# Scheduling the RWKV recurrence steps ahead of all other ready work in a two-block fp32 kernel

## The chip, the cores and the metric

The kernel runs on one core of a Trainium2 chip. The metric is the device time of one execution in microseconds (us). Before the change the median of three runs is 2998.11 us (2994.8 to 3004.18). About 0.3%, 9 us, is what a measurement of this kernel can tell from no change.

## The reference

One launch computes two transformer-like blocks on a 256 x 1024 fp32 input `x`. The first block is: a SwiGLU feed-forward, a mixing stage, and a second SwiGLU. Its mixing stage is what matters here:

```
h = rms_norm(x, mix_norm)
p_rwkv, p_q, p_k, p_v, p_gate = split(h @ w_in)
y_a = rwkv7_time_mix(p_rwkv, ...)          # 16 heads of 64, a recurrence over 256 steps:
                                           #   state = state*w + (state@a) b^T + v k^T ; out = state @ r
y_b = dilated_attention(p_q, p_k, p_v)     # 3 groups of 4 heads
merged = g_a * (y_a @ w_proj_rwkv) + g_b * (y_b @ w_proj_attn)     # g = sigmoid(p_gate + b_gate)
x = x + merged @ w_out
```

The second block has two layers, each with three branches (mLSTM, differential attention, Fourier) and a SwiGLU. All their modulation rows come from products `silu(c) @ w_ada`; those of its first layer are computed during the first block's mixing stage.

## The kernel before

Every large matrix product goes through weight blocks. `weights` (line 194) loads a block `wr` of 128 x 1024 or 128 x 512 numbers from HBM by a DMA in the queue of SP (SyncE), ScalarE (ACT) rounds it to `wh` (line 201), VectorE (DVE) forms the rest `wl = wr - wh` (line 202), and TensorE (PE) multiplies three times: by lines 213 to 215 into `g` where tokens are the rows of the result, by lines 248 to 250 where tokens are its columns. A block of the first kind feeds 12 matmuls. There are four buffers of `wr` and three each of `wh` and `wl`.

In the mixing stage `first_block` (line 994 and below) builds generators, each a piece of work cut into steps by `yield`. The string PLAN names the generator whose next step is written out: "0" and "1" are the two halves (8 heads each) of the RWKV recurrence, "k" the keys, receptances and values of the second half, "a" the dilated attention, "g" the gates, "r" the modulation rows (`ada`, line 1105, which multiplies `wa`, 512 KB each).

A half's recurrence is a chain. `rwkv_prep`: decay products (`pz`, `pa`, `pl`, `px`, `pe`, lines 543 to 565), elementwise work on DVE (lines 575 to 603: `kk`, `XA`, `eL`, `em`, `bon`), copies to `WV` and `GB` by 20 small DMAs (lines 612 to 617), transposes `tr` (line 626) with their copies `AR` and `BK`. `rwkv_solve`: products `gr` (line 666) masked into `GB` on DVE (lines 671, 673), four transposes `FS` (line 686), 31 rounds of forward substitution on DVE (`fsp` line 695, `T` line 697), products `pq` and `pr2` (lines 713, 718), and for each of two token tiles `p` (lines 767, 777, 792), the state products `pf` (lines 817, 819), normalisation and the gate product `pg` (lines 750, 751). Token shifts (`pv`, `pr`, lines 475 to 477) precede each half.

PLAN does not fix the order in which an engine executes. The program's layer has a scheduler that walks the written program: of the instructions that are ready by its own reckoning it takes the one with the smallest priority number, which is normally the place in the written program. The result is one fixed queue for each engine, in which an instruction that waits holds up all behind it; PE and SP likewise. The rows of such queues are shown below for the change.

## Time and profile before

| what | value |
|---|---|
| median of three runs | 2998.11 us |
| the profiled execution's own time | 2999.31 us |
| its span, first to last instruction | 2997.5 us |
| PE busy, matmuls | 2890.7 us, 96% |
| PE busy, weight loads | 2429.5 us, 81% |
| DVE, ACT busy | 1775.0 us, 59%; 1178.6 us, 39% |
| data moved by DMA | 409.57 MB, mean 137 GB/s |
| mixing stage's recurrences | about 253 to 613 us of the span |

A row of a timeline begins with its start in us from the span's start and its length; a value in square brackets is how long the engine sat idle before it, and what ended that. `PEclk` is the share of full speed that TensorE was granted. The trace records a matmul of these fp32 products as two entries, so that `x4` in a timeline of PE is two instructions.

### The profile page before, as it was taken

How to read it: one execution, taken by the hardware profiler on the slowest of the kernel's cores; microseconds unless marked ns; L12 is line 12 of the kernel's file. 1: busy time of each engine (PE TensorE's matmuls, PEld its weight loads, DVE VectorE, ACT ScalarE, POOL GpSimd, SP SyncE). 2: the span in 40 equal slices, each digit the busy share in tenths (PEclk: the TensorE clock that was granted, in tenths of full speed). 3: DMA queues.
4: the chain of work that ended last, by engine and by line, in shares of the span. 5: the costliest groups of instructions: out<-in, count | busy, mean ns of one | idle time of the engine just before them, and what ended most of it. 6: DMA issues, size and time to landing. Idle time of an engine off the chain costs nothing.

```text
span 2997.5 us, 42457 instructions
## 1 busy us (share of the span) xinstructions
PE 2890.7 (96%) x16704; PEld 2429.5 (81%) x16704; DVE 1775.0 (59%) x3036; ACT 1178.6 (39%) x1943; POOL 98.4 (3%) x265
## 2 busy tenths in 40 slices
PE   8999999998999999999999999999999999999998
PEld 7987676767997888987788987877778897799797
DVE  5557847446555445436784266777665555665665
ACT  4444333334443334325442333222344444444443
POOL 1010000002000000000000001000020000000000
PEclk9999989889999999999999999999999999999999
DMA  6656737346664222231233254555442243255564
GB/s 199 188 160 202 237 117 216 101 144 206 185 186 127 64 71 64 72 104 51 64 118 105 85 169 146 159 173 155 148 140 85 85 140 101 78 152 169 169 189 141
DMA packets 291441, 409.57 MB, mean 137 GB/s; under 512 B 30757, under 2 KB 182181, under 8 KB 291242
## 3 DMA queue, kind: packets, MB, share of 16 engines
q1 hardware_dynamic: 291242, 406.87, 44.5%
q8 instruction: 131, 2.15, 0.3%
q14 instruction: 68, 0.56, 0.1%
HBM read 396.98 MB, written 3.24 MB: 134 GB/s over the span
## 4 chain that ended last, share of the span: by engine, by line
PE 82%; DVE 8%; issue 3%; ACT 3%; POOL 2%; DMA 2%; SPq 0%; ACTq 0%; POOLq 0%; DVEq 0%
PE g L214 12%; PE g L215 11%; PE g L213 11%; PE g L248 10%; PE g L250 10%; PE g L249 10%; DVE wl L202 2%; PE dC L1363 2%; PE tr L316 1%; PE ada L1105 1%; PE I L1339 1%; ACT dae L1460 1%; PE pf L817 1%; PE f L1530 1%; PE pf L819 1%
## 5 line engine op out<-in xcount | busy, mean ns | idle before, releaser
L202 DVE TENSOR_TENSOR wl<-wr,wh 128x1024 fp32r<-128x1024 f32 (+1 forms) x606 | 733.6, 1212 | 717.3 <-ACT wh L201 714.8
L201 ACT CAST wh<-wr 128x1024 fp32r<-128x1024 f32 (+1 forms) x606 | 630.8, 1042 | 1061.0 <-PE g L215 494.5
L214 PE MATMUL g<-wl,xh 128*128 128x512 f32 (+2 forms) x1880 | 733.2, 390 | 12.5 <-DVE wl L202 12.5
L213 PE MATMUL g<-wh,xh 128*128 128x512 f32 (+2 forms) x1880 | 731.1, 392 | 9.6 <-ACT wh L201 5.8
L248 PE MATMUL g<-xh,wh 128*128 128x256 f32 (+1 forms) x2352 | 726.7, 309 | 3.8 <-ACT wh L201 3.1
L215 PE MATMUL g<-wh,xl 128*128 128x512 f32 (+2 forms) x1880 | 727.6, 388 | 0.0
L250 PE MATMUL g<-xh,wl 128*128 128x256 f32 (+1 forms) x2352 | 722.8, 307 | 1.9 <-DVE wl L202 1.9
L249 PE MATMUL g<-xl,wh 128*128 128x256 f32 (+1 forms) x2352 | 723.1, 307 | 0.0
L248 PEld LDWEIGHTS g<-xh,wh 128*128 128x128 f32 x2352 | 452.8, 193 | 34.7 <-issue 6.7
L250 PEld LDWEIGHTS g<-xh,wl 128*128 128x128 f32 x2352 | 452.5, 192 | 30.5 <-issue 7.3
L249 PEld LDWEIGHTS g<-xl,wh 128*128 128x128 f32 x2352 | 452.9, 193 | 26.5 <-issue 7.0
L214 PEld LDWEIGHTS g<-wl,xh 128*128 128x128 f32 x1880 | 359.2, 191 | 90.6 <-DVE wl L202 20.3
L213 PEld LDWEIGHTS g<-wh,xh 128*128 128x128 f32 x1880 | 357.1, 191 | 88.3 <-ACT wh L201 9.7
L215 PEld LDWEIGHTS g<-wh,xl 128*128 128x128 f32 x1880 | 358.8, 191 | 74.7 <-issue 5.7
L1155 DVE SCALAR_TENSOR_TENSOR aa<-wa,cond,aa 128x512 f32<-128x512 f32 x168 | 114.8, 744 | 4.0 <-DMA wa<-in_w_ada_dram 4.0
L303 ACT CAST xh<-tr 128x256 fp32r<-128x256 f32 (+1 forms) x114 | 50.4, 462 | 131.7 <-PE tr L316 116.2
L1460 ACT ACTIVATE dae<-sc,dast 128x512 f32<-128x512 f32 (+1 forms) x96 | 58.5, 614 | 42.2 <-DVE dast L1458 37.3
L304 DVE TENSOR_TENSOR xl<-tr,xh 128x256 fp32r<-128x256 f32 (+1 forms) x114 | 57.5, 529 | 22.6 <-ACT xh L303 22.2
L1458 DVE TENSOR_REDUCE dast<-sc 128x1 f32<-128x512 f32 (+1 forms) x96 | 53.8, 596 | 24.2 <-PE sc L1457 23.8
L316 PE MATMUL tr<-ident,hn 128*128 128x128 f32 x160 | 28.7, 316 | 39.6 <-DVE hn L345 20.2
L316 PEld LDWEIGHTS tr<-ident,hn 128*128 128x128 f32 x160 | 22.4, 163 | 47.6 <-DVE hn L343 20.6
L330 POOL TENSOR_SCALAR rn_s<-rn_s 128x1 f32<-128x1 f32 x20 | 11.2, 560 | 1209.8 <-ACT junk L329 849.0
(392 smaller groups left out, 2676.9 us busy)
## 6 DMA issues: line engine op xcount, KB each, us to landing
wr<-in_w_in_dram SPq DMA_DIRECT2D x156, 512.0 KB
wr<-in_ffn_w_in_dram SPq DMA_DIRECT2D x88, 512.0 KB
wr<-in_w_ffn_in_dram SPq DMA_DIRECT2D x84, 512.0 KB
wr<-in_w_in_dram SPq DMA_DIRECT2D x156, 256.0 KB
wr<-in_w_ffn_out_dram SPq DMA_DIRECT2D x50, 512.0 KB
wa<-in_w_ada_dram SPq DMA_DIRECT2D x48, 512.0 KB
wa<-in_w_ada_dram SPq DMA_DIRECT2D x96, 256.0 KB
wr<-in_ffn_w_out_dram SPq DMA_DIRECT2D x44, 512.0 KB
```

What stands on the lines that cost most here:

```text
L201: nc.scalar.copy(out=wh[:, :kn, :ntot], in_=src)
L202: nc.vector.tensor_tensor(out=wl[:, :kn, :ntot], in0=src, in1=wh[:, :kn, :ntot].bitcast(F32), op=ALU.subtract)
L213: nc.tensor.matmul(o_, xh, wh[:, n0:n1], start=(kc == 0), stop=False)
L214: nc.tensor.matmul(o_, xh, wl[:, n0:n1], start=False, stop=False)
L215: nc.tensor.matmul(o_, xl, wh[:, n0:n1], start=False, stop=(kc == nk - 1))
L248: nc.tensor.matmul(o_, wh[:, fs], xh, start=(kc == 0), stop=False)
L249: nc.tensor.matmul(o_, wh[:, fs], xl, start=False, stop=False)
L250: nc.tensor.matmul(o_, wl[:, fs], xh, start=False, stop=(kc == nk - 1))
L316: self.nc.tensor.transpose(p[:, j * P:(j + 1) * P], src[:, (c + j) * P:(c + j + 1) * P], self.ident)
L1155: nc.vector.scalar_tensor_tensor(out=y, in0=raw, scalar=self.cond[:, k, s:s + 1], in1=acc[s], op0=ALU.mult, op1=ALU.add)
L1363: nc.tensor.matmul(pc[:, 0:257], kw[:, kc * P:(kc + 1) * P], V[t][:, 0:257], start=True, stop=True)
L1460: nc.scalar.activation(out=em, in_=ps[:, 0:n], func=AF.Exp, bias=st[:, m:m + 1], scale=1.0, accum_out=st[:, 2 + m:3 + m])
```

## The change

Each step of the generators "0" and "1" is written out under `high_priority()`, which sets the priority number to that of the program's start for the instructions emitted inside it and restores it afterwards. Nothing is computed differently. Lines behind the edit are numbered two higher in the changed kernel.

```
             for x in PLAN:
-                next(fills[x], None)
+
+                with self.tc.high_priority() if x in "01" else ExitStack():
+                    next(fills[x], None)
```

Each engine has the same instructions as before. The sequence of the weight blocks (`wr`, `wh`, `wl`, 606 of each) is the same on SP, ACT and DVE. Only what stands between them moves, and only in one piece: on PE about 1500 instructions from matmul number 1426 on, up to the first half's last transposes, on DVE about 500. Everything before and after stands as it did. Counted in weight blocks that DVE has split before it, no step of a recurrence moves by more than five places: the first half's `GB` (line 671) from 90 to 87, its 19th round of substitution from 94 to 89, its `TB` (line 701) stays at 100, the second half's first round of substitution stays at 118, and the last state update (line 829) stays at 129.

DVE, first half, from the end of the key norm (`kn_y`) to the end of the elementwise chain. Before:

```order
L202 TENSOR_TENSOR wl<-wr,wh 128x1024
L297 SCALAR_TENSOR_TENSOR kn_y<-kn_w,kn_y 128x16
L582 TENSOR_TENSOR kk<-kk,kn_y 128x1024
L585 SCALAR_TENSOR_TENSOR XA<-kk,ex 128x512 x2
L202 TENSOR_TENSOR wl<-wr,wh 128x1024
L587 SCALAR_TENSOR_TENSOR kk<-ta,kk 128x1024
L629 COPY AR<-tr 128x8x64
L589 SCALAR_TENSOR_TENSOR kk<-kk,em 128x1024
L590 SCALAR_TENSOR_TENSOR ta<-ta,kar 128x1024
L202 TENSOR_TENSOR wl<-wr,wh 128x1024 x2
```

The same place after:

```order
L202 TENSOR_TENSOR wl<-wr,wh 128x1024
L295 TENSOR_TENSOR kn_w<-kn_y 128x16
L296 SCALAR_TENSOR_TENSOR kn_w<-kn_w,n_2410 128x16
L297 SCALAR_TENSOR_TENSOR kn_y<-kn_w,kn_y 128x16
L582 TENSOR_TENSOR kk<-kk,kn_y 128x1024
L475 TENSOR_TENSOR pv<-pv,pr 128x1024
L585 SCALAR_TENSOR_TENSOR XA<-kk,ex 128x512 x2
L476 TENSOR_TENSOR pv<-pv,mu 128x1024
L587 SCALAR_TENSOR_TENSOR kk<-ta,kk 128x1024
L477 TENSOR_TENSOR pr<-pr,pv 128x1024
L589 SCALAR_TENSOR_TENSOR kk<-kk,em 128x1024
L590 SCALAR_TENSOR_TENSOR ta<-ta,kar 128x1024
```

The weight block that stood inside the chain now stands behind it, and the token shift of the values (lines 475 to 477), which stood ahead of it, runs inside it.

SP, first half, where the copies to `WV` and `GB` and the loads `wa` stand. Before:

```order
L194 DMA wr<-in_w_in_dram 128x2x512 x4
L612 DMA WV<-pr 64x512 x4
L194 DMA wr<-in_w_in_dram 128x2x256
L616 DMA GB<-kk 64x4x64 x8
L194 DMA wr<-in_w_in_dram 128x2x256
L617 DMA GB<-em 64x4x64 x8
L1101 DMA wa<-in_w_ada_dram 128x1024 x2
```

After, from the last loads that stand ahead of the copies:

```order
L194 DMA wr<-in_w_in_dram 128x2x512 x3
L612 DMA WV<-pr 64x512 x2
L616 DMA GB<-kk 64x4x64 x4
L612 DMA WV<-pr 64x512
L616 DMA GB<-kk 64x4x64 x2
L612 DMA WV<-pr 64x512
L617 DMA GB<-em 64x4x64 x6
```

Three weight loads that stood ahead of the ten loads `wa` (92 before them in all) now stand behind them (89). In the second half two more weight loads than before stand ahead of the copies.

PE, first half, the state products of the first 64-step chunk of the second token tile. Before, its eight pairs of `pf` stand behind `pg` and follow each other with nothing between (the rows show the first pair):

```order
L750 MATMUL pg<-g_3198,lg 128x512
L751 MATMUL pg<-g2b,lg 128x512
L817 MATMUL pf<-WV,GB 128x64
L819 MATMUL pf<-S,RG 128x64
```

After, six weight matmuls stand between the first four pairs (the rows begin with the last of them) and the other four:

```order
L817 MATMUL pf<-WV,GB 128x64
L819 MATMUL pf<-S,RG 128x64
L250 MATMUL g<-xh,wl 128x256
L248 MATMUL g<-xh,wh 128x256
L249 MATMUL g<-xl,wh 128x256
L250 MATMUL g<-xh,wl 128x256
L248 MATMUL g<-xh,wh 128x256
L249 MATMUL g<-xl,wh 128x256
L817 MATMUL pf<-WV,GB 128x64
```

What follows moves too: 58 weight matmuls stand directly behind the eighth pair, where 3 did. Behind the attention's transposes that come next stand 72, where 12 did; the second chunk's pairs come after those.

## Rows read from the trace of the kernel before

**Rows 1.** The page: the span, and each engine's busy time.
```profile
span 2997.5 us, 42457 instructions
PE 2890.7 (96%) x16704; PEld 2429.5 (81%) x16704; DVE 1775.0 (59%) x3036; ACT 1178.6 (39%) x1943; POOL 98.4 (3%) x265
```

**Rows 2.** Windows, the recurrences' stretch: length, busy by engine, PEclk, DMA share, GB/s.
```profile
253.00:613.00 360.00, 345.06 (x2215) 248.38 (x2214) 238.41 (x538) 126.48 (x240) 3.81 (x11) 0.89 0.54 164
```

**Rows 3.** Waits of PE in 253 to 613 us: total, times, longest.
```profile
PE g L214 <- DVE wl L202: 6.0, 4, 2.8
PE g L213 <- ACT wh L201: 5.3, 4, 2.2
...
PE pq L713 <- DVE drs_w L296: 0.8, 1, 0.8
```

**Rows 4.** Windows inside that stretch, columns as in rows 2.
```profile
265.00:280.00 15.00, 10.83 (x43) 8.25 (x42) 11.19 (x21) 7.25 (x10) 0.00 (x0) 0.77 0.78 263
280.00:320.00 40.00, 39.26 (x238) 27.14 (x240) 38.03 (x63) 10.72 (x17) 1.64 (x4) 1.00 0.75 227
320.00:330.00 10.00, 5.43 (x33) 4.60 (x26) 8.94 (x27) 2.90 (x5) 0.42 (x1) 0.83 0.61 191
...
380.00:400.00 20.00, 20.00 (x96) 12.23 (x95) 7.61 (x11) 7.01 (x13) 0.00 (x0) 0.74 0.35 112
...
420.00:455.00 35.00, 35.00 (x157) 25.97 (x156) 16.50 (x39) 8.55 (x15) 0.00 (x0) 0.71 0.28 77
455.00:485.00 30.00, 28.88 (x179) 20.99 (x175) 24.77 (x45) 7.13 (x13) 0.00 (x0) 1.00 0.68 203
485.00:500.00 15.00, 12.01 (x46) 6.88 (x46) 14.35 (x57) 6.13 (x11) 0.00 (x0) 0.89 0.55 184
...
550.00:613.00 63.00, 62.94 (x344) 44.15 (x344) 28.38 (x83) 17.24 (x47) 0.20 (x4) 0.73 0.23 76
```

**Rows 5.** Timeline of DVE in the first half.
```profile
279.80 1.23 DVE L582 TENSOR_TENSOR kk<-kk,kn_y 128x1024 f32<-128x1024 f32 x1
281.06 1.29 DVE L585 SCALAR_TENSOR_TENSOR XA<-kk,ex 128x512 f32<-128x512 f32 x2
...
298.68 0.41 DVE L671 TENSOR_TENSOR GB<-gr,kbase 128x256 f32<-128x256 f32 x1
...
305.60 3.72 DVE L686 STREAM_TRANSPOSE FS<-GB 32x1024 f32<-32x1024 f32 x3
...
316.47 0.19 DVE L695 TENSOR_TENSOR fsp<-FS,T 128x30 f32<-128x30 f32 x1
...
324.75 0.29 DVE L695 TENSOR_TENSOR fsp<-FS,T 128x128 f32<-128x128 f32 x1
```

**Rows 6.** Timeline of PE in the first half.
```profile
270.04 0.73 PE L213 MATMUL g<-wh,xh 128*128 128x512 f32 x2 [2.24 <-ACT wh L201]
272.71 0.79 PE L214 MATMUL g<-wl,xh 128*128 128x512 f32 x1 [1.93 <-DVE wl L202]
...
282.04 0.60 PE L626 MATMUL tr<-ident,XA 128*128 128x128 f32 x4
...
283.15 0.40 PE L213 MATMUL g<-wh,xh 128*128 128x512 f32 x1
...
286.33 0.40 PE L215 MATMUL g<-wh,xl 128*128 128x512 f32 x1
...
307.15 1.03 PE L1105 MATMUL ada<-wa,cond 128*2 128x512 f32 x4 [0.69 <-DMA wa<-in_w_ada_dram]
...
322.44 0.50 PE L213 MATMUL g<-wh,xh 128*128 128x256 f32 x2 [1.81 <-ACT wh L201]
...
325.69 0.58 PE L214 MATMUL g<-wl,xh 128*128 128x256 f32 x1 [2.75 <-DVE wl L202]
```

**Rows 7.** Timelines of SP's queue and of ACT around the loads `wa`.
```profile
304.02 9.84 SPq L1101 DMA_DIRECT2D wa<-in_w_ada_dram  x8
313.92 27.41 SPq L194 DMA_DIRECT2D wr<-in_w_in_dram  x16
...
321.77 1.32 ACT L201 CAST wh<-wr 128x512 fp32r<-128x512 f32 x2 [5.53 <-DMA wr<-in_w_in_dram]
```

## The prediction

> **What bounds the kernel now.** I read the page's busy times first: TensorE's matmuls cover 96% of the span and no other engine comes near [rows 1]. So time is won only where TensorE waits or runs slowly. The change reorders one piece, so next I read a window over the stretch in which that piece executes, 253 to 613 us [rows 2]. TensorE is busy for 345.06 of its 360 us: 14.9 us idle. Its mean granted clock is 0.89, so about 360 x 0.11 = 39.6 us went to the lower clock. These two numbers, 54 us together, are all that any order of the same instructions could give back.
>
> The waits of TensorE in that stretch say what it waits for [rows 3]: 11.3 of the 14.9 us are for weight blocks, `wl` from VectorE (6.0) and `wh` from ScalarE (5.3). A recurrence's own product (`pq`, by a step that shares VectorE with it) accounts for 0.8. TensorE therefore does not wait for the recurrence; it waits for the weight stream that shares VectorE with it. That decides the case: work on the recurrence's chain is given an order that it hardly lacked, at the cost of the stream that does bound.
>
> The windows show where the 39 us of clock lie [rows 4]. Each loses its length times (1 - clock): 3.5 (265 to 280), 1.7 (320 to 330), 5.2 (380 to 400), 10.2 (420 to 455), 1.7 (485 to 500), 17.0 (550 to 613), 39.2 in all. Three of them (6.8 us) hold idle TensorE. The other 32.4 us fall where TensorE is busy throughout with `pf`, `p`, one-row and two-column products, small work of the recurrences and of `ada`.
>
> **The Trainium skill on the clock.** "TensorE: Matmul & The Clock Gate", section "HAM oscillation — how this bites in real kernels", says that gaps in which TensorE idles bring the lower clock, and that matmuls should stay back to back. The trace agrees for 6.8 us and not for 32.4 us, where there is no gap to name. By the rule alone each new wait of some us would add a fall like that of 320 to 330 us and nothing could be won elsewhere; that speaks against this change.
>
> **The change part by part.** No instruction is added, so the sum holds only waits and clock.
>
> *The end.* The last steps of the second half stand where they did in the weight stream, and so does everything behind them. The chain is not what the next stage waits for: both orders end the stretch at the same matmul. That term is 0.
>
> *268 to 275 us.* TensorE waits 2.24 us for `wh` and 1.93 for `wl` [rows 6]. In the new order the square `sq` goes ahead of two of ScalarE's exponentials, and one 1024-wide token-shift operation no longer stands ahead of the first `wl`. A 1024-wide operation takes 1.23 us [rows 5]. I take 1.2 off the second wait and 0.5 off the first: -1.7. Bounds: 0 and -4.2.
>
> *The elementwise chain.* Between three weight blocks and the next, VectorE now executes seven 1024-wide operations, two 512-wide ones and three short ones: 7 x 1.2 + 1.2 + 3 x 0.2 (the 30-element step took 0.19) = 10.2, and 1.2 for the next `wl`: 11.4 us [rows 5]. TensorE has cover for part of it. A block is 12 matmuls at 0.227 us (14 steps from 283.15 to 286.33) = 2.7 us [rows 6]. Three blocks are 8.2, of which 2.4 pass while the later two are split; eight transposes take 0.9 (282.04 to 283.15 less one matmul), and two matmuls of the next block, which need `wh` only, 0.5. That is 7.2 us, so a new wait for `wl` of about 4 us, near 280 us. Bounds: 0 (the prep runs sooner than I think) and 10.
>
> *The substitution.* Before, TensorE waits 0.69, 1.81 and 2.75 = 5.25 us between 307 and 326 us [rows 6]. The cause is in the queue of SyncE: the weight loads go behind eight `wa` (9.84 us of issue), and the first arrives 7.9 us after the queue reaches it, at 321.77 [rows 7]. Now three weight loads more stand behind `wa`. The `wa` themselves start some 4 us sooner, so the first block behind them should land near 317 us and TensorE meets VectorE instead. There the `BK` copies of the second tile stand behind four pairs of `GB` masks (8 x 0.41 = 3.3 us), for which `gr` waits about 3 us. Then come four `FS` (1.24 each), during which `gr`, `ada` and one block cover. Then 17 rounds without a weight block: 15 took 8.28 us from 316.47 to 324.75, so 9.4; with two 1024-wide shifts ahead (2.4), two short steps (0.4) and the `wl` (1.2), 13.4 us [rows 5]. Against it stand ten matmuls (2.3), twelve `ada` at 0.5 (1.03 for two) and two of the next block, 8.9 us [rows 6]: a wait of 4.5. So 7.5 for 5.25: +2.3. Bounds: -5.25, and +8.4 if the twelve `ada` (6.2) arrive too late to cover.
>
> *The first `pq`.* 27 more weight matmuls stand ahead of it, so its wait of 0.8 [rows 3] goes: -0.8.
>
> *The second half.* Its steps keep their places to within three blocks. The windows 455 to 500 us hold 1.1 + 3.0 = 4.1 us of idle [rows 4]; two weight loads more stand ahead of the copies, for which I take -1.5 (0 to -4.1).
>
> *The clock.* In 420 to 455 us, 10.2 us were lost. There 58 and 72 dense weight matmuls now stand in blocks between the small products. I take 4 of it, between 0 (the same small products come in some order anyway) and 10.2. The new wait near 280 us costs a fall like that of 320 to 330: +1.7. Of the 17.0 and 5.2 I take nothing, since the runs of `pf`, `p` and `pz` there are much the same in both orders.
>
> Sum: -1.7 + 4.0 + 2.3 - 0.8 - 1.5 - 4.0 + 1.7 = 0.0. So the profiled execution's 2999.31 us stays; it is 1.2 above the median of the runs shown, 2998.1, which is therefore the forecast: 2998 us.
>
> **The rivals.**
>
> *The weight stream starves (slower).* One mechanism: VectorE is a fixed queue, and the chain put first in it delays `wl`. For it: the three waits above, and VectorE is busy 38.0 us of the 40 before 320 us [rows 4], so nothing is caught up there. Price: the elementwise wait at its upper bound (+6 over what I took) and the substitution's at its own (+6.1), and no gain of 4 from the clock: about +16, 3014 us. It decides once TensorE's waits between 265 and 330 us, now 4.2 + 5.25 = 9.4, pass some 20. Against it: `ada` and the transposes lie beside the chain. The skill's rule, by which each of these waits brings a fall of the clock, would add 2 to 3 falls at 1.7 us.
>
> *The small products are spread out (faster).* For it: most of the clock's loss sits on runs of small products without a gap, and the first half's `pf` are now split by weight matmuls. If 420 to 455 us keep the full clock and half of the 17.0 of 550 to 613 goes, the clock gives 18.7 in place of 4: about -15, 2983 us. Against it: the second half's order hardly changes.
>
> *The change does next to nothing.* The scheduler took the recurrences' steps almost as soon as they were ready before; no step moves by more than five weight blocks and most by none or one. Then every term above is near 0 and the time is 2998 us, the same as the forecast's.
>
> **How the numbers follow.** Under 0.3%, 9 us, a measurement of this kernel cannot tell. The forecast has 0.40 and the change that does nothing 0.14, both within it. The spread of small products has 0.24, for the clock holds the largest sum and no row tells how it would answer. The starved stream has 0.22. So faster 0.24, the same 0.54, slower 0.22. The range takes in both rivals but for their far ends: 2982 to 3013 us. The forecast's own range is 2990 to 3006.
>
> **What would show it.** Right: matmul idle of 13 to 18 us in the recurrences' stretch; a wait of `g` for `wl` near 280 us of about 4 us; the one behind the substitution named `wl` and not a DMA; a mean clock of 0.88 to 0.92 in the stretch; and the stretch 360 us long within 8. Wrong: idle over 25 us there (the stream starves), or a clock above 0.93 (the small products matter more than I take), or any difference that arises after 613 us, where both orders are one.

## The result and the profile after

The changed kernel takes 3028.44 us, the median of 6 runs (3015.54 to 3035.81). The kernel before takes 3000.9 us beside it (6 runs, 2994.8 to 3006.43). The ratio is 1.0085 with an interval of 1.0066 to 1.0103: 27 us slower. The forecast was 2998 us in a range that ends at 3013 us, so it missed.

The profiled execution took 3035.81 us, near the slow end of its runs. The page's first lines answer to [rows 1]:

```profile
span 3034.0 us, 42452 instructions
PE 2916.3 (96%) x16704; PEld 2442.4 (81%) x16704; DVE 1777.3 (59%) x3036; ACT 1178.3 (39%) x1943; POOL 98.3 (3%) x265
```

The span grew by 36.5 us against [rows 1]. TensorE's busy time grew by 25.6 us with the same 16704 instructions in it. More busy time for the same instructions means that they ran more slowly. The clock records of the traces show two levels, full (2.4 GHz) and half (1.2 GHz). The mean granted clock, first before and then after:

```profile
core 0: 2997.5 us, clock 0.975
core 0: 3034.0 us, clock 0.966
```

So 3034.0 x 0.0336 = 102 us went to the lower clock against 75 before (clocks to four digits from these records): 27 of the 36.5 us.

The next rows are windows of the changed kernel, first over the whole stretch (253 to 644 us answers to 253 to 613 in [rows 2]), then inside it, as in [rows 4]. Columns: start and end, length, busy time and instructions of PE, PEld, DVE, ACT, POOL, then PEclk, DMA share, GB/s.

```profile
253.00:644.00 391.00, 369.44 (x2226) 261.28 (x2227) 241.56 (x538) 127.13 (x241) 3.82 (x11) 0.84 0.49 151
268.00:280.00 12.00, 9.60 (x41) 7.10 (x40) 9.92 (x19) 8.07 (x12) 0.00 (x0) 0.86 0.87 285
320.00:335.00 15.00, 9.88 (x51) 8.02 (x48) 12.16 (x38) 5.43 (x8) 0.00 (x0) 0.77 0.41 115
...
420.00:440.00 20.00, 20.00 (x93) 17.26 (x93) 5.71 (x11) 3.98 (x7) 0.00 (x0) 0.66 0.30 97
437.10:454.20 17.10, 15.94 (x125) 13.57 (x124) 10.14 (x24) 9.31 (x14) 0.00 (x0) 1.00 0.56 158
450.00:480.00 30.00, 28.84 (x103) 20.58 (x102) 15.54 (x30) 7.60 (x15) 0.00 (x0) 0.60 0.43 121
516.00:573.00 57.00, 54.80 (x488) 37.92 (x486) 40.11 (x109) 24.21 (x56) 1.04 (x2) 1.00 0.59 182
573.00:590.00 17.00, 17.00 (x81) 10.42 (x80) 5.38 (x12) 1.23 (x4) 0.00 (x0) 0.60 0.37 121
607.00:644.00 37.00, 37.00 (x147) 28.83 (x147) 15.66 (x46) 10.32 (x27) 0.20 (x4) 0.54 0.04 15
```

The stretch, up to the same matmul in both, is 31 us longer. TensorE is idle for 21.6 us of it against 14.9: +6.7. Its mean clock is 0.84 against 0.89: 391 x 0.16 = 62.6 us lost against 39.6, +23. From 516 to 573 us the clock is at its full level, so the loss sits in separate places, among them 450 to 480 us (30 x 0.40 = 12 us), 573 to 590 (6.8) and 607 to 644 (17.0). In the last two TensorE has no idle time at all: 17.00 us busy of 17.00, 37.00 of 37.00.

The longest of TensorE's waits in the stretch answer to [rows 3]; the columns are the same:

```profile
PE g L214 <- DVE wl L202: 5.4, 3, 3.4
PE g L213 <- ACT wh L201: 4.5, 3, 2.1
PE ada L1107 <- DMA wa<-in_w_ada_dram: 4.1, 3, 2.8
PE tr L882 <- DVE dsq L875: 3.1, 2, 1.7
PE pz L543 <- DMA w<-in_rwkv_w_dram: 1.4, 1, 1.4
```

Waits for `wl` and `wh` are 11.0 us in all with 1.1 us at line 250, against 11.5 before (11.3 and 0.2 at line 250): no more than there were. The waits for `wa` loads grew from 1.1 to 4.1 us. New are the 1.3 us in which `gr` waits for `BK`, the wait at the first `pz` and those for `dsq` (before, `tr` waited 1.2 us for another step of VectorE).

The last piece of the second half's recurrence shows what happens inside a low place. Two timelines of PE (start, duration, instruction). First the kernel before, behind its third `pg`:

```profile
577.54 0.43 PE L819 MATMUL pf<-S,RG 64*128 64x64 f32 x2
577.90 1.59 PE L1105 MATMUL ada<-wa,cond 128*2 128x512 f32 x4
579.42 0.69 PE L817 MATMUL pf<-WV,GB 128*128 128x64 f32 x2
...
583.13 1.87 PE L1105 MATMUL ada<-wa,cond 128*2 128x512 f32 x4
...
592.87 0.43 PE L817 MATMUL pf<-WV,GB 128*128 128x64 f32 x2
```

Such a group of `pf` takes 0.43 us at the full clock and 0.69 at the lower one. The clock falls at 578 us, and `ada` stands twice between the `pf`. By 592 us `pf` takes 0.43 us again. Now the changed kernel, at the same place:

```profile
607.46 0.44 PE L819 MATMUL pf<-S,RG 64*128 64x64 f32 x2
607.83 0.69 PE L817 MATMUL pf<-WV,GB 128*128 128x64 f32 x2
...
611.53 1.89 PE L1107 MATMUL ada<-wa,cond 128*2 128x512 f32 x8
...
617.36 0.69 PE L819 MATMUL pf<-S,RG 64*128 64x64 f32 x2
...
627.06 0.69 PE L819 MATMUL pf<-S,RG 64*128 64x64 f32 x2
```

Sixteen of these groups follow each other without `ada`, which comes as a block of eight entries behind them; two sets of eight `pf` groups follow, with `sc`, `tr`, `po` and a few weight matmuls between. The clock falls at 607.8 us, and at 627 us `pf` still takes 0.69 us. By the clock records the lower level lasts here until 641.9 us, 34.1 us at a stretch; before, the same work had 13.7 and 10.2 us with 3.4 us at the full clock between.

Six other orders of the next section pass the same place, one profile each. With sixteen groups ahead of `ada`, as here, the lower level lasts 27.3 us (second half only; steps behind the solve). With eight groups ahead of the first `ada` and `ada` twice between, it lasts 30.7 us (steps to the solve; all others) and 37.5 us (with `ada`'s steps). With six groups ahead of it, as before, it lasts 10.2 us (first half only). So `ada` between the groups is not enough for a short fall; the short ones go with the six groups ahead of the first. That is read from these traces and not tested.

### The profile page after: what moved, and what is told of

The parts are those of the page before. It is cut to its first block, busy times and chain, and to the rows that moved or that the text cites. A ratio compares the mean times of both kernels' runs of the same rounds, so it can differ in the third digit from the quotient of the medians.

```text
span 3034.0 us, 42452 instructions
## 1 busy us (share of the span) xinstructions
PE 2916.3 (96%) x16704; PEld 2442.4 (81%) x16704; DVE 1777.3 (59%) x3036; ACT 1178.3 (39%) x1943; POOL 98.3 (3%) x265
## 4 chain that ended last, share of the span: by engine, by line
PE 80%; DVE 8%; issue 4%; ACT 3%; POOL 2%; DMA 2%; SPq 0%; ACTq 0%; POOLq 0%; DVEq 0%
PE g L214 11%; PE g L215 11%; PE g L213 11%; PE g L248 10%; PE g L250 10%; PE g L249 10%; DVE wl L202 2%; PE dC L1365 2%; PE tr L316 1%; PE ada L1107 1%; PE I L1341 1%; PE pf L817 1%; PE pf L819 1%; POOL rn_w L291 1%; ACT dae L1462 1%
## 5 line engine op out<-in xcount | busy, mean ns | idle before, releaser
L214 PE MATMUL g<-wl,xh 128*128 128x512 f32 (+2 forms) x1880 | 735.0, 391 | 11.3 <-DVE wl L202 11.3
L248 PEld LDWEIGHTS g<-xh,wh 128*128 128x128 f32 x2352 | 455.4, 194 | 39.6 <-issue 11.0
L249 PEld LDWEIGHTS g<-xl,wh 128*128 128x128 f32 x2352 | 455.5, 194 | 29.3 <-issue 9.6
L316 PEld LDWEIGHTS tr<-ident,hn 128*128 128x128 f32 x160 | 21.8, 160 | 47.6 <-DVE hn L343 20.7
L1107 PE MATMUL ada<-wa,cond 128*2 128x512 f32 x192 | 49.9, 630 | 4.1 <-DMA wa<-in_w_ada_dram 4.1
```

The lines of the kernel that those rows point to most:

```text
L214: nc.tensor.matmul(o_, xh, wl[:, n0:n1], start=False, stop=False)
L248: nc.tensor.matmul(o_, wh[:, fs], xh, start=(kc == 0), stop=False)
L249: nc.tensor.matmul(o_, wh[:, fs], xl, start=False, stop=False)
L316: self.nc.tensor.transpose(p[:, j * P:(j + 1) * P], src[:, (c + j) * P:(c + j + 1) * P], self.ident)
L1107: nc.tensor.matmul(p[32 * j:32 * j + 2, :], self.cond[:, k, :], raws[j], start=False, stop=(k == KD - 1))
```

## The experiments

The theories: **clock** (the new order strings small products together, so TensorE spends more time at 1.2 GHz), **waits** (DVE and the DMA queue give weights and `wa` later), **chance** (any new order meets the clock differently). The ratio is to runs of the kernel before that were taken beside it. In this table the loss is span x (1 - mean clock), the rest is span x mean clock, both medians over the runs of a kernel. The clock is given to three digits, so each is good to some 2 us.

| kernel | us (runs) | ratio, interval | loss | rest |
|---|---|---|---|---|
| before | 3002.0 (88) | 1 | 78.0 | 2921.9 |
| changed | 3028.4 (6) | 1.0085, 1.0066 to 1.0103 | 99.9 | 2926.8 |
| first half only | 3014.9 (6) | 1.0045, 1.003 to 1.006 | 90.5 | 2922.4 |
| second half only | 3005.5 (11) | 1.0016, 1.0007 to 1.0025 | 84.0 | 2921.7 |
| steps to the solve | 3013.3 (5) | 1.0039, 1.0024 to 1.0054 | 84.4 | 2924.8 |
| steps behind it | 3022.9 (5) | 1.0082, 1.0065 to 1.0098 | 93.7 | 2927.5 |
| all others | 3062.4 (5) | 1.0204, 1.0186 to 1.0221 | 116.3 | 2944.3 |
| changed, with `ada`'s steps | 3031.3 (6) | 1.0099, 1.0078 to 1.012 | 95.4 | 2933.5 |
| wide `pf`, before | 2956.2 (4) | 0.9846, 0.9824 to 0.9868 | 48.7 | 2906.0 |
| wide `pf`, changed | 2982.9 (4) | 0.9936, 0.9913 to 0.9959 | 73.0 | 2909.6 |
| gathered `pf`, before | 2978.4 (6) | 0.9914, 0.9896 to 0.9932 | 64.0 | 2913.5 |
| gathered `pf`, changed | 3008.6 (12) | 1.0016, 0.9992 to 1.004 | 85.8 | 2921.5 |
| `pf` by turns, before | 2965.3 (4) | 0.987, 0.9857 to 0.9883 | 54.8 | 2907.8 |
| `pf` by turns, changed | 3003.0 (12) | 1.0004, 0.999 to 1.0018 | 81.1 | 2918.1 |
| wide products added, before | 3017.5 (12) | 1.0045, 1.0023 to 1.0068 | 70.9 | 2944.8 |
| wide products added, changed | 3037.5 (6) | 1.0117, 1.0091 to 1.0143 | 80.4 | 2955.0 |

The first two lines already divide the 27 us: 22 lost clock, 5 everything else. The 88 runs of the kernel before go from 2992 to 3010 us and the six of the changed one from 3016 to 3036, so chance from run to run does not make the difference. That does not answer the third theory, by which each order has a clock of its own without a rule. Against it speaks only that all seven new orders of the same products (the changed one, its four parts, the opposite and the one with `ada`'s steps) lose more than before, none less; the seven are akin, so it stays a rival.

**Parts of the change.** Four kernels give the priority to some steps only.

```diff
-with self.tc.high_priority() if x in "01" else ExitStack():
+with self.tc.high_priority() if x == "0" else ExitStack():     # first half; second half: x == "1"
```

> Only the first half's recurrence steps (x == "0") run with the priority; the second half's stand as before. Clock theory (the small products are strung out over longer stretches, TensorE stays at its lower clock there): the first half's chain lies at 270 to 480 us of the changed kernel, where 61 us were at the lower clock against 38 before, so about half of the clock's 22 us loss in the stretch comes with it: 1.003 to 1.006 of before, with the low intervals near 454 to 478 us in the profile, while the stretch behind 600 us looks as before. Wait theory (weights late behind a fixed queue): nearly all waits of the first half (elementwise 1.6, substitution 7.0 us) are here too, and that alone would make 1.001 to 1.002, with TensorE's idle 16 to 18 us and the clock as before. Chance theory (any new order meets the clock differently): anything between 0.995 and 1.009.

> Only the second half's steps (x == "1") run with the priority. Clock theory: the low intervals at 608 to 642 and 656 to 676 us of the changed kernel (54.5 us, against 31.3 us of the like places before) come from the second half's small products; so 1.003 to 1.006, and with the first half's alone the two add up to about 1.0085. Wait theory: the second half's waits grew by some 4 us only: 1.001. If the two halves add up to much less or more than 1.0085, neither half carries the loss and it depends on how the two meet.

```diff
+n = done[x] = done.get(x, 0) + 1
-with self.tc.high_priority() if x in "01" else ExitStack():
+with self.tc.high_priority() if x in "01" and n <= 9 else ExitStack():   # to the solve; behind it: n > 9
```

> Priority for steps 1 to 9 of each half only: token shifts, elementwise chain, Gram products, forward substitution, first solve products. The token tiles (p, RG, pf, norm) have none. Wait theory: the waits for weights come from this part, so it carries the whole difference: 1.007 to 1.009. Clock theory: the low intervals lie in the token tiles' small products, so this part costs its waits alone, 3 to 7 us: 1.001 to 1.003, with a clock of 0.975 as before.

> Priority for the steps behind the solve only (from the tenth on: token tiles' p, RG, pf, norm); the chain up to it stands as before. Clock theory: these steps hold most of the small matmuls (pf, tr), so the loss is here: 1.005 to 1.008, clock near 0.967. Wait theory: VectorE's queue ahead of the weights is as before through the substitution, so 1.000 to 1.002. If both this and the run with the other steps are near 1, the loss needs the chain to start earlier and its tiles to follow.

All four are slower than before. The first half alone costs 0.45%, in the clock theory's band (and in the wide one of chance). The second costs 0.16%, below that band and near the wait theory's number; but its rest did not grow (-0.2 us), its loss did (+6.0), so it is the clock, and less of it than I said. The steps to the solve cost 0.39%, between the two theories' numbers, with 6.4 us of loss and 2.9 of rest. The steps behind it cost 0.82%, just above the clock theory's band (0.5 to 0.8%) and far above the wait theory's: nearly the whole change. The halves add up to 0.61%, the two groups of steps to 1.21%, the change is 0.85%. So the parts do not add up and no one step carries the loss, but in each of the four the clock is the larger account.

Where the falls lie is another matter. I had expected the first half's low places near 454 to 478 us. Its profile has 10.2 us there, and falls of 13.7 us at 298 and at 352 us. Up to 389 us of the changed kernel both have the same sequence of matmuls on TensorE; still the clock differs, first the first half only, then the changed kernel:

```profile
290.00:320.00 30.00, 28.72 (x156) 17.61 (x153) 26.45 (x54) 2.92 (x6) 1.86 (x4) 0.77 0.79 254
290.00:320.00 30.00, 28.10 (x169) 16.14 (x167) 29.25 (x58) 3.17 (x6) 2.07 (x4) 1.00 0.82 262
```

TensorE waits 1.3 us here in the first and 1.9 in the second, so no longer wait brings that fall. The same order can meet the clock differently from one execution to another, and one profile does not tell where an order loses; only sums over several runs compare.

**The opposite change.**

```diff
+with self.tc.high_priority() if x not in "01" else ExitStack():
```

> The opposite change: priority for the other pieces of the plan (everything but the two recurrences), the recurrences' steps without. If the loss is that the recurrences' small products are taken as soon as they are ready and so strung out in small groups between weight matmuls, then holding them back gathers them: clock theory with gathering good gives 0.990 to 1.000 of before, clock 0.976 to 0.98. If gathered small products are as bad (a long run of them alone drops the clock too), 1.000 to 1.008. Wait theory: the weights stand first on VectorE, so the waits of 11.3 us for wl and wh go down to 4 to 8, 0.997 to 0.999, unless the recurrence's chain becomes so late that the end of the stretch waits for it (over 1.01, with TensorE idle there).

1.0204, far from both numbers of the clock theory. The exception that I gave to the wait theory came true in part: over 1.01, with TensorE idle for 46 us of the stretch (253 to 680 us; before 14.9), 19 of them for steps of the recurrence's chain and 17 for `wa`. But the loss is 38 us above before's and the rest 22 us, so the clock is again the larger account, and more than the clock theory gave at worst (1.008). The longest waits of the stretch:

```profile
PE ada L1107 <- DMA wa<-in_w_ada_dram: 16.6, 11, 5.9
PE tr L626 <- DVE XA L585: 6.9, 1, 6.9
```

Some loads of these steps also moved to the program's start, so this run is a change of more than the stretch. Holding the small products back in this way does not help.

**What brings the clock down.** The first probe runs the products by themselves, each segment behind 130 dense weight-like matmuls.

> A measurement by itself, with the whole computation left out (the input is copied to the output): after 130 dense weight-like matmuls (128x512, single pass) each time, runs of the small products alone and mixed with 256-column weight-like matmuls. Clock theory, as read from the two traces: the clock falls where small fp32 products run with few weight matmuls between (110 pairs of 64-column products alone; 4 pairs and 6 weight matmuls by turns), and stays at 1.0, or falls for less than 4 us at a time, where there are many (4 pairs and 24; 16 pairs and 72); TensorE is busy above 90% in all of them. If instead idle gaps alone bring the lower clock, every segment without a gap stays at 1.0. The two wide fp32 segments (65 and 128 rows of input) tell whether the number of rows filled matters: unknown, I expect both at 1.0. The two-column products (weights of 128x2, 512 columns moved, 80 alone, or one per 7 weight matmuls): unknown; in the changed kernel they stood at both levels.

Windows of the probe: the dense run, `pf` pairs alone, 4 pairs and 6 weights by turns, 4 and 24, 16 and 72, 128-row products of 512 columns, two-row ones. There is no DVE column here. The probe's other two kinds, wide products of 65 rows and 7 weight matmuls to one two-row product, kept 1.00.

```profile
5.20:37.00 31.80, 31.77 (x132) 26.17 (x132) 0.00 (x0) 0.00 (x0) 1.00 0.08 30
36.80:170.00 133.20, 133.20 (x442) 107.72 (x440) 0.00 (x0) 0.00 (x0) 0.51 0.00 0
201.10:311.00 109.90, 109.90 (x398) 93.32 (x397) 0.00 (x0) 0.00 (x0) 0.51 0.00 0
341.50:402.50 61.00, 61.00 (x361) 56.10 (x361) 0.00 (x0) 0.00 (x0) 0.83 0.00 1
432.00:514.00 82.00, 82.00 (x409) 72.41 (x408) 0.00 (x0) 0.00 (x0) 0.69 0.00 1
612.60:652.20 39.60, 39.60 (x94) 17.59 (x93) 0.00 (x0) 0.00 (x0) 1.00 0.00 0
681.70:699.00 17.30, 17.30 (x162) 4.12 (x161) 0.00 (x0) 0.00 (x0) 1.00 0.00 1
```

The pairs alone run at 0.51 for 133.20 us, in which TensorE is busy for 133.20 us. So there need be no gap for the clock to fall. Six weight matmuls to four pairs do not help (0.51); 24 do (0.83). Of 16 and 72 I had expected falls under 4 us; they were 17 us long each time (0.69 over the segment). Wide products and two-row ones keep 1.00. The Trainium skill names gaps as the cause ("TensorE: Matmul & The Clock Gate", section "HAM oscillation — how this bites in real kernels"); this segment has none, so the measurement differs from it and decides.

The second probe has the same work in four orders: 64 pairs, 16 two-row products, 96 weight-like ones.

> A measurement by itself; the whole computation is left out. Four segments have the same work (four cycles of 16 pairs of 64-column fp32 products as pf's, 4 two-row products as ada's, 24 weight-like matmuls of 256 columns) in four orders: gathered (16 pairs, then the 4, then the 24); one two-row product after every 4 pairs, then the 24; 6 weight matmuls after every 4 pairs, then the 4; both between. Clock theory, order matters: gathered loses most; from the first probe (16 pairs and 72 weights: 1.07 us at the lower clock for a pair; 4 and 24: 0.57) I expect gathered about 65 to 80 us at the lower clock, all between 35 to 65, the two others in between. If the order of the same work does not matter to the clock, the four are alike within 7 us. Then four segments of one product alone, fp32, by width: 128 rows and 64 columns (as pf's first; low nearly throughout), 128x128 (as a transpose), 64 rows and 128 columns (as p), 128x256. Expected: the low share falls with the number of columns; 256 columns at full clock; the 64-row one no different from the 128-row one.

In turn: gathered, two-row products between, weights between, both between; then 128-row products of 64 columns alone, and 64-row ones of 128 columns alone.

```profile
37.10:128.00 90.90, 90.90 (x386) 71.42 (x385) 0.00 (x0) 0.00 (x0) 0.62 0.00 1
157.30:245.40 88.10, 88.10 (x386) 59.49 (x385) 0.00 (x0) 0.00 (x0) 0.81 0.00 1
274.70:376.40 101.70, 101.70 (x386) 80.15 (x384) 0.00 (x0) 0.00 (x0) 0.54 0.00 0
407.10:489.20 82.10, 82.10 (x386) 56.74 (x385) 0.00 (x0) 0.00 (x0) 0.88 0.00 1
518.50:554.30 35.80, 35.80 (x322) 35.80 (x321) 0.00 (x0) 0.00 (x0) 1.00 0.00 1
640.10:667.20 27.10, 27.10 (x242) 26.96 (x241) 0.00 (x0) 0.00 (x0) 1.00 0.01 1
```

The same instructions take 82.1 to 101.7 us by their order alone, and length x (1 - clock) is 34.5, 16.7, 46.8 and 9.9 us; the time at the lower clock is twice that. Gathered came as expected (69 us), both between better than expected (20). Weights between were to lie in the middle and are the worst: six weight matmuls to four pairs, as in the first probe. What helps here is the two-row product every four pairs. `ada` stands between the `pf` in the order before as well, and no longer at 607 us after. But the three orders that have `ada` there behind eight groups, which is four pairs, keep the long fall, so the kernel does not bear it out. And 64 columns alone do not bring the clock down, against what was expected: 1.00.

**What in a pair does it.**

> A measurement by itself; the whole computation is left out. 80 pairs each of 64-column fp32 products: a 128-row and a 64-row one that accumulate (rows 0-63, then rows 64-127), two 128-row ones that accumulate, two 64-row ones that accumulate, the 128/64 pair without accumulating, two 64-row ones, rows 0-63 and 64-127 by turns, and the accumulating 128/64 pair with its halves gathered by 4 and by 8. The earlier probes: the pair alone is at the lower clock from 3.5 us after its start, one 128-row product after another stays at the full clock. Theory change of rows (TensorE drains when the number of rows it reads changes): 128/64 slow and low with and without accumulating, 128/128 and 64/64 at the full clock, gathering by 4 or 8 brings the full clock. Theory accumulation (the second product of a pair waits for the first one's sum): all accumulating pairs low, whatever their rows, the others at the full clock, and gathering helps as well.

In turn: 128/64 rows accumulating, 128/128, 64/64 on the same half, 128/64 apart, 64-row products by turns of the two halves, gathered by eight (by four it is 0.52 over 72.90 us).

```profile
37.50:133.20 95.70, 95.70 (x322) 77.41 (x320) 0.00 (x0) 0.00 (x0) 0.52 0.00 0
291.60:327.50 35.90, 35.90 (x322) 35.86 (x322) 0.00 (x0) 0.00 (x0) 1.00 0.00 1
357.00:420.50 63.50, 63.50 (x322) 63.38 (x321) 0.00 (x0) 0.00 (x0) 0.54 0.00 1
451.60:548.10 96.50, 96.50 (x322) 78.02 (x321) 0.00 (x0) 0.00 (x0) 0.52 0.00 0
676.70:694.80 18.10, 18.10 (x322) 18.03 (x321) 0.00 (x0) 0.00 (x0) 1.00 0.01 2
829.40:897.80 68.40, 68.40 (x322) 66.14 (x320) 0.00 (x0) 0.00 (x0) 0.53 0.00 1
```

Accumulation is out: 128/128 accumulate at 1.00, 128/64 apart run at 0.52. The theory of the change of rows holds for the pair only; 64/64 on one half and the gathered ones were to be at the full clock and are at 0.52 to 0.54. So neither theory stands, and what it is in these products stays open. By the length over 320 records, a record takes 0.299 us (128/64), 0.112 (128/128), 0.198 (64 rows, one half), 0.057 (64 rows, by turns). The Trainium skill says that a weight load overlaps a running product when the two use different groups of rows ("TensorE: Matmul & The Clock Gate", "Part 3: Packing small matmuls — row/col tiling"); that 64-row products by turns take half of the 128-row ones' time, both at the full clock (0.057 and 0.112), agrees with it, though the run does not show that it is this overlap.

**Is pf the difference?** Three pairs of kernels, each edit in both orders. First `pf` with 256 columns and one head's matrix:

```diff
-for pair in range(4): ...matmul(p[:, 64 columns], GBf[head], WV[head]) ; ...matmul(..., RG[pair], S[pair])
+nc.tensor.matmul(o_, GBf[:, eidx(par), c, 64:192], WV[t][:, c].rearrange("p (a b) k -> p b a k", b=2)[:, par], ...)
+if ch: nc.tensor.matmul(o_, RG[rows, 0, c].rearrange("p s k -> p (s k)"), S[rows], start=False, stop=True)
```

> The kernel before, with every four 64-column products of pf replaced by one of 256 columns (same number of columns streamed, one head's stationary matrix for all four, so the other heads' products are left out and the outputs differ). 168 products fewer. Clock theory: pf's runs no longer bring the clock down; of the 39 us that the lower clock costs in the stretch some 15 to 25 come back, with the shorter work itself 25 to 45 us: 2955 to 2978 us. If pf is not what brings the clock down: only the work goes, about 20 us, 2980 us, and the lost time stays at 75.

> The changed kernel with the same replacement. Clock theory: with pf's small products gone the two orders differ by little more than the waits: 3 to 12 us between this one and the kernel before with the same replacement, where the two whole kernels differ by 25 to 27. Wait theory, or a clock that some other product brings down: the difference stays at 20 to 30 us.

Then the same sums with the four 128-row products first:

```diff
+for pair in range(4): matmul(o_(pair), GBf[head], WV[head], start=(pair == 0), ...)
+for pair in range(4 if ch else 0): matmul(o_(pair), RG[pair], S[pair], start=False, stop=(pair == 3))
```

> The kernel before, with pf's products gathered by kind: the four 128-row ones, then the four 64-row ones, in place of four pairs (the same sums). Whichever of the two theories holds, pf's runs become shorter and bring the clock down less: of 75 us lost to the lower clock 10 to 25 come back, and pf itself takes less; 0.985 to 0.996 of before. If neither holds (it is the 64 columns after all, or the total of small work): 0.997 to 1.003.

> The changed kernel with the same gathering. If pf carries the difference of the two orders, this one comes within 10 us of the kernel before with the same gathering. By the run with 256-column products, where the difference stayed at 26.7 us, I expect the difference to stay: 18 to 30 us, nearly all of it lost clock outside pf.

And with both tiles of sums open, the 64-row products by turns of the halves:

```diff
+for par in range(2):
+    for pair in range(4): matmul(ps[par](pair), GBf[head], WV[head], ...)
+for pair in range(4 if ch else 0):
+    for par in range(2): matmul(ps[par](pair), RG[rows(par), pair], S[rows(par), pair], ...)
```

> The kernel before, with pf's eight 128-row products first and then the eight 64-row ones, rows 0-63 and rows 64-127 by turns (two PSUM tiles open at once; the same sums). By the probe of pairs, 16 products (32 records) as pairs take 32 x 0.299 = 9.6 us at the lower clock, gathered by eight 32 x 0.214 = 6.8 us at the lower clock, and apart 16 x 0.112 + 16 x 0.057 = 2.7 us at the full clock. In this order four or five of the six sets stand by turns in full. Row theory: pf's falls go; 0.982 to 0.990 of before, below the run with gathered products (0.9914), lost clock 45 to 58 us. If the gathering already gave all there is, 0.990 to 0.993.

> The changed kernel with the same edit; here only about half of the sets stand by turns in full, since the priority lets the first four of a set go ahead. If the two orders differ because TensorE is nearer to a fall of the clock for longer in the new one (pf being only a part of it), the difference to the kernel before with the same edit stays at 15 to 30 us; 0.992 to 1.000 of before. If pf carries it, under 10 us.

`pf` does bring the clock down: each edit takes 14 to 29 us off the loss of the kernel before. But the difference of the two orders stays. Loss and rest, changed less before, are 24.3 and 3.6 us (wide), 21.8 and 8.0 (gathered), 26.3 and 10.3 (by turns), against 21.9 and 4.9 unedited. The clock theory's number for the wide pair, 3 to 12 us, was wrong (26.7, in the band for waits or a clock that some other product brings down; 24.3 of it is clock), and with it the theory that `pf` alone carries the difference. The other two were expected to stay apart and did, by 30 us and by 38, the last more than expected. These two pairs are the weaker test, for `pf` is not cured in them: gathered by four it ran at 0.52 in the probe, and with the changed order's priority only about half of the sets stand by turns in full (the 64-row products take 15.2 us there, 11.2 in the order of before).

No edit left the other products where they were. With the entries of `pf` left out, the sequence of TensorE's matmuls in the traces differs from that of the unedited kernel in some 20 (wide), 6 (gathered) and 107 (by turns) of 16480 entries for the order of before, and in some 170 to 360 for the changed one. So the scheduler's new order is part of each of these results.

Where the loss sits with `pf` by turns is seen in windows of the same length at like places: the `ada`, score and value products of the attention in the middle, and the run behind the third `pg`. First the kernel before with the edit, then the changed one.

```profile
470.00:498.00 28.00, 24.99 (x111) 13.59 (x109) 22.44 (x83) 12.88 (x32) 0.00 (x0) 0.94 0.66 209
555.00:586.00 31.00, 30.52 (x211) 23.07 (x210) 23.98 (x68) 13.61 (x33) 0.20 (x4) 1.00 0.18 61
```

```profile
481.00:509.00 28.00, 23.75 (x62) 10.50 (x62) 18.80 (x74) 8.74 (x21) 0.00 (x0) 0.51 0.54 183
587.00:618.00 31.00, 30.43 (x150) 24.24 (x149) 16.38 (x46) 12.09 (x32) 0.20 (x4) 0.67 0.17 55
```

In both places the changed order is low where the other is at or near the full clock (0.51 and 0.94, 0.67 and 1.00). The second has `pf` in fours in the changed order, so it shows no more than that. The first has no `pf` at all. It follows waits of 1.6 and 2.4 us for `wa`; then come `tr`, `sc` and `po` of the attention with few weight blocks between. So in the first the clock is low on the attention's small products behind a wait; whether the products or the wait hold it there is not tested apart.

**Wide products put back.**

```diff
 p = self.t("pf")
+for _ in range(2): nc.tensor.matmul(p[0:2, 256:512], self.ident[:, 0:2], XA[t][:, 1, 0:256], start=True, stop=True)
 po = self.t("po")
+nc.tensor.matmul(po[0:2, 128:512], self.ident[:, 0:2], V[0][:, 0:384], start=True, stop=True)
```

> The changed kernel with idle products added and nothing taken out: ahead of each of pf's 16 tiles of sums two fp32 products of two columns of weights and 256 moved columns, ahead of each of the 12 attention value products one of 384, into columns that nobody reads. By the full-clock rate of ada's products in the first probe (17.3 us for 80 of 512 columns, 0.217 us each) they are some 32 x 0.11 + 12 x 0.16 = 5.4 us of work. In the probe of orders one such product after every four pairs halved the time at the lower clock (34 against 68 us). Clock theory: the lost clock falls from some 99 us to 75 to 88, and the kernel with more work is no slower or faster: 3005 to 3028 us. If the clock falls for another reason (waits), the work is paid in full or more: 3033 to 3040 us, clock 0.966.

> The kernel before with the same added products, as a control. Clock theory: here ada's products stand among pf's already, so less is to be had: 2990 to 3006 us, clock 0.974 to 0.980; the two orders come nearer to each other than 27 us. If the waits bring the falls: 3006 to 3010 us, and the difference to the changed order with the same products stays at 27 us or more.

The loss of the changed kernel falls by 19.5 us, to 80.4, inside the clock theory's band; that of before falls by 7.1. The difference of the two losses goes from 21.9 to 9.5 us. The price was mis-sized: the rest grew by 28 and 23 us, not 5.4. I had taken it from `ada`'s products in the probe, which go to four places of the output by turns; the added ones all go to one. That this makes the difference in price is not tested. So both kernels became slower, at a clock of 0.974 and 0.976: the time of the changed one is in the wait theory's band and its clock is not, and the 3017.5 us of the other lie above both bands. The group of the added `pf` products in the changed kernel (count, busy us, mean ns of a record):

```profile
L815 PE MATMUL pf<-XA,ident 128*2 128x256 f32 x64 | 19.1, 423 | 0.2 <-ACT WV L783 0.2
```

Runs of both kernels scatter by 29 to 37 us, so 9.5 is rough; the direction is what counts. With more work, TensorE loses less to its clock. That wide products among the small ones do this is argued and not shown, for the order changed too: with all `pf` and `po` left out, some 410 of 16088 entries stand elsewhere than in the kernel without the added products, and the changed kernel's six weight matmuls within a set of `pf` no longer stand there. A last one moves `ada` itself:

```diff
+with self.tc.high_priority() if x in "01" or x == "r" and n > 1 else ExitStack():
```

> The changed kernel, with the priority for the two-row products' steps (x == "r", from the second on: ada and its loads) as well, so that they stand nearer to where the plan has them among the recurrences' steps; by the order one of the second half's three runs of pf has ada in it again, and one of the first half's. Clock theory: part of the loss comes back, 1.003 to 1.007 of before. Wait theory: the loads of ada move ahead of the weights on SyncE, so the waits grow: 1.008 to 1.012.

1.0099. The loss fell by 4.5 us only, and the rest grew by 6.7: in this order one of the second half's three runs of `pf` had `ada` in it again, and the early loads of `wa` cost waits elsewhere. The time is in the wait theory's band: here waits do weigh, since the loads of `wa` go ahead of the weights. And in the run of `pf` that has `ada` in it again the lower level lasts 37.5 us, where the changed kernel has 34.1: putting `ada` back behind eight groups did not bring the clock back there. That speaks against its place as the cause by itself.

**The version that beats both.** The kernel before with `pf` by turns takes 2965.3 us, 0.987 of before: 38 us less than the runs beside it. Its two groups of `pf` products, then those of the kernel before (count, busy us, mean ns):

```profile
L815 PE MATMUL pf<-WV,GB 128*128 128x64 f32 x128 | 18.1, 293 | 0.0
L820 PE MATMUL pf<-S,RG 64*128 64x64 f32 x96 | 11.2, 304 | 0.0
```

```profile
L817 PE MATMUL pf<-WV,GB 128*128 128x64 f32 x128 | 29.5, 336 | 0.0
L819 PE MATMUL pf<-S,RG 64*128 64x64 f32 x96 | 26.4, 366 | 0.0
```

The two groups take 29.3 us in place of 55.9. By the table 23 us of the gain are lost clock and 14 the rest.

## Why the prediction was wrong, point by point

- **What bounds.** Right that TensorE does, and that idle time and clock are the two accounts. Wrong in the conclusion that the weight stream is the one that decides. I drew it because the waits can be read one by one; the clock account was 39.6 of the 54 us and I had no row that told how it answers to order.
- **The end, 0.** Held: both orders end the stretch at the same matmul, and the step of 31 us stands at 644 us. Behind it the profiled run lost some 3 us more in the next 90 us, in the same order of work. Profiles of the other kernels lost 5 to 17 us there (before 8.5, changed 11.9), so scatter can make that; one profile cannot show more. The sign that I had named, a difference that arises after 613 us, is there all the same: 5.5 of the 36.5 us.
- **268 to 275 us, -1.7.** Left are 2.4 of 4.2 us: -1.8. Right in the sum; nearly all of it came off the second wait (1.6) and little off the first (0.2), where I had 1.2 and 0.5.
- **The elementwise chain, +4.0.** 1.6 us for `wl` and 0.3 for `kk`: a wait there, half the size.
- **The substitution, +2.3.** 0.6, 1.3, 1.7 and 3.4, together 7.0 us for 5.25; I said 7.5. The size is right, the reason half: the last wait is named `wl`, but the load came at 321.05 us, not 317 (ACT waited 25.15 us for it), so the DMA is late as well.
- **The first pq, -0.8.** 0.5 is left: -0.3.
- **The second half, -1.5.** Wrong sign: with all of the above and 1.4 us at the first `pz`, the 6.7 us of added idle leave about +3.7 here: `ada` waits up to 2.8 us for `wa` and `tr` twice for `dsq`. I had said that its steps keep their places; its neighbours did not.
- **The clock, -4.0 and +1.7. This is the step that failed.** It measured about +22 in the medians, +23 in the stretch of the profile. The waits' terms sum to +2.3 and measured +6.7 in the profile, about +5 in the medians, so it is the clock that was mis-sized, and in its sign. Two steps of it are wrong. From "58 and 72 dense weight matmuls now stand in blocks between the small products" I took a gain of 4. The weights did run at the full clock for most of their length (1.00 from 437.1 to 454.2 us in the windows of the first section), but the small products on either side of them lost more: the lower level lasts 13.7 us over the `pf` ahead of the blocks and into the first of them, and 23.9 us over the one-row `ada` and the `pf` behind them, where before three falls of 6.8 us lay between 421 and 452 us. Nor were dense blocks new there: before, 75 weight matmuls stood together at 404 to 413 us, ahead of the tile's last products. And six weight matmuls inside a set of `pf` are near the order that the probe shows to be the worst of all. The other step is "the runs of `pf`, `p` and `pz` there are much the same in both orders", by which I took nothing of the 17.0: the products are the same, but `ada` went from between them to behind them, and 17.0 us of loss from 550 us on became 6.8 + 17.0. Which change of order brings which fall is not shown (with `ada` back between the groups the fall there was no shorter); the runs show the sum, about 22 us of clock in place of a gain of 2.3.
- **The rivals.** The starved stream decides if the waits between 265 and 330 us pass 20 us; they are 11.3, so slower came true by another way, and the forecast had no rival by which the clock gets worse. The faster rival took the right quantity, the spread of the small products, and the wrong sign.
- **The range.** It left the clock's upper side out: I bounded its term by 0 and -10, though the stretch already lost 39.6 us to it and the order of its products was what changed.
- **The signs.** Of those for being right, idle (21.6 us, not 13 to 18), the wait near 280 us (1.6, not 4), the clock (0.84, not 0.88 to 0.92) and the length of the stretch (391 us, not 360) failed, and the wait behind the substitution is named `wl` as I said. None of those for being wrong was a clock below 0.88.

Open is how the loss divides among the places of the stretch: the parts do not add up, and the profile shows one execution of a loss that differs from run to run (0.966 to 0.972 over six runs of the changed kernel). The sum, that the clock takes about 22 of the 27 us, rests on the medians of all runs.

## What to carry to other kernels

Before moving small matmuls, look at what stands between them: in windows at full busy time the granted clock tells whether a run of them holds 2.4 GHz, and a new order can cost more there than all its waits. Price such a change by a probe with the same work in the two orders, since busy share and instruction count see nothing of it. Put accumulating products of unequal row counts in groups by rows, and the half-height ones by turns of the halves: in the kernel before, the first gave 0.9% and both together 1.3%, with what the scheduler moved besides. And expect an edit of a few products to move others too: compare the queues before giving a result to the edit.

## What the hardware showed that I had not expected

- TensorE at 100% busy runs at a mean clock of 0.51 for 133 us, so almost wholly at 1.2 GHz, on alternating 128- and 64-row products of 64 columns, and at 2.4 GHz on 128-row ones of the same width.
- 64-row products of 64 columns take 0.198 us a record at a clock of 0.54 on one half of the rows and 0.057 us at 1.00 by turns of the halves.
- Two-row products of 512 columns hold the full clock; one after every four pairs halved the loss (16.7 for 34.5 us), while six 256-column weight matmuls in that place raised it.
